# The beginning of a block kernel: tokens in two halves, and modulation in pieces between them

## The chip, the cores and the metric

The kernel runs on one core of a Trainium2 chip. The metric is the device time of one execution in microseconds (us); the number given for a kernel is the median of its runs. A core has five engines with a queue of instructions each, which are worked off in order: PE (TensorE, matrix products; its weight loads are shown apart as PEld), DVE (VectorE), ACT (ScalarE), POOL (GpSimd) and SP (SyncE, which here only issues DMAs). Engines wait for one another by semaphores.

## What is computed

One layer of a diffusion trunk, of 1024 latent tokens (a grid of 16 rows by 64 columns) and 256 context tokens, all of width 1024, in float32. Cut to what matters here:

```python
mod_x = silu(c) @ w_mod + b_mod           # six vectors of 1024: sh1, sc1, gt1, sh2, sc2, gt2
mod_c = silu(c_ctx) @ w_mod + b_mod
h_x = rmsnorm(x, g_pre_mix) * (1 + sc1) + sh1       # (1024, 1024)
h_c = rmsnorm(ctx, g_pre_mix) * (1 + csc1) + csh1   # (256, 1024)
u, q, k, v = split(h_x @ w_in)            # four times (1024, 512); k, v of h_c too
mix = concat(pool_mixer(u), neighbourhood_attention(q, k, v, k_c, v_c, rpb)) @ w_out
x = x + gt1 * rmsnorm(mix, g_post_mix)
y = square(relu((rmsnorm(x, g_pre_mlp) * (1 + sc2) + sh2) @ w_mlp_in)) @ w_mlp_out
out = x + gt2 * rmsnorm(y, g_post_mlp)
```

What is changed lies before the first products `h_x @ w_in`: the sums of squares and roots of `rmsnorm`, the turning of x so that its 1024 channels lie on the partitions, the product of `silu(c)` with the first two vectors' columns of `w_mod`, and the first of the sums for u.

## The kernel before

**Pieces.** A token tile `x0` to `x7` holds 128 tokens by 1024 channels. A channel chunk k (0 to 7) holds 128 channels on the partitions. `xT[k]` is chunk k of all 1024 tokens, in two halves b of 512 columns. The columns are ordered by grid tiles: (m, r, c), 8 tiles m of 16 rows by 8 columns; half b=0 holds grid tiles 0 to 3. In the memory the tokens are ordered by grid rows, so a token tile is two grid rows, and each half of `xT` needs all eight token tiles.

**Products** are made in three passes: weights and activations are split in a high part (type fp32r) and a low part (the rest), and high×high, low×high and high×low are summed (`some_sums`, L449). `hx[b][k]` holds both parts of the modulated half b of chunk k, 512 columns each. `pus[b][j]` is the bank in which the product for columns j (128 of u) and half b is summed over k.

**Steps in the beginning**, all in one order by hand: within `in_order` every engine keeps the order in which the program names the instructions.

- SP issues the loads: x0 to x7 (512 KB each, L293), then for each pair of chunks q (0 to 3) four pages `wm` of modulation weights (L300; 128 partitions with four runs of 1 KB) and a page of `w_in` (L178), then the context.
- `squares` (ACT, L131) sums the squares of a token tile; DVE adds epsilon (L136), POOL takes the root (L140), and DVE scales the tile in `normalised` (L334).
- PE turns 128 by 128 blocks (`turned`, L346) into banks `pxt`; ACT and DVE copy them into `xT` in the order of grid tiles (`by_bands`, L353). `spare` (L341) are transpositions of the unit matrix into a free place; nothing reads them.
- `mod_sums` (L401): the vector `sT` (32 columns, two of them used: c and c_ctx) times 256 columns of `w_mod` for shift and scale, the 1024 channels summed in four groups of 32 rows of the array, 32 instructions for a pair of chunks. `mod_kept` copies the row (ACT, L406), `shift_scale` picks it on PE with `pck` (L418) and makes the columns `a1` (scale) and `s1` (shift) on DVE (L422 to L427).
- `latent(b, k)` makes `hx` (`modulated`, L205 to L210): for b=0 ACT writes the high part, DVE the exact value and then the low part.
- The loop over q sums u for both chunks of a pair and both halves, and between them makes the next pair's modulation, weights and `hx`. For b=1 only columns j = 0, 1 are summed in it; j = 2, 3 come after the loop.

After the loop the context, k and v, pooling, attention, the output product and the MLP follow. They are long rows of matrix products; `stored_sum` (L519) adds quarters of the modulated `xT`, and the additions at L550 make it anew for k = 0 and 1 of half 0, since those two were modulated into another place.

**Banks.** PSUM has eight banks of 512 columns. `ps1` has six (tag `mm`), `ps_t` two (tag `T`, `lasting`). The function `bank` gives one of the two lasting ones to names that begin with `pm` and to a few others. A bank is given to a new name when every instruction that uses the old one is done.

Of the kernel before, what the change touches and what calls it, by code (L numbers as in the profile page):

```python
# [11 lines left out]
F32 = mybir.dt.float32  # L12
F32R = mybir.dt.float32r
# [5 lines left out]
P = 128  # L19
D = 1024  # L20
KT = D // P
# [48 lines left out]

def _pick_table():
# [9 lines left out]
def hybrid_block(ctx, tc, x, ctx_in, w_mod, b_mod, gp1, gp2, w_in, pool_w, rpb, w_out, w1, w2, vectors,  # L81
# [37 lines left out]
    tiles = lambda a: a.rearrange("(r m c) d -> m r c d", r=QR, m=NM)  # L119
# [151 lines left out]
    with tc.tile_pool(name="ps1", bufs=6, space=PSUM) as ps1, tc.tile_pool(name="tmp1", bufs=3) as tmp:  # L271

        def bank(name):
            if name[:2] == "pm" or name in ("pxt1_0", "pxt0_2", "pxt1_7", "pct2", "pct3"):
                return lasting(name)
            return ps1.tile([P, 512], F32, tag="mm", name=name)
# [20 lines left out]
        def mod_load(q, kh, w):  # L297
            src = w_mod[:, w * D + q * 256 : w * D + (q + 1) * 256].rearrange("(h k p) f -> h p k f", p=P, h=2)
            t = page(f"wm{q}_{kh}_{w}")
            nc.sync.dma_start(t.rearrange("p (k f) -> p k f", k=4), src[kh])  # L300
            return t

        xn = [token_tile(f"x{n}", x[n * P : (n + 1) * P, :]) for n in range(NT)]
        wm, raw_u = [], []
        for q in range(4):
            wm.append([[mod_load(q, kh, w) for w in range(2)] for kh in range(2)])
            raw_u.append(load(f"wu{q}", pair(w_in, q, 0, 512)))
# [17 lines left out]
        inverse = {}  # L325

        def squares(name, t):
            jk = page(f"jk{name}")
            ms = sm(f"ms_{name}", 1, 4)
            mean_square(jk, t, ms)  # L330
            inverse[name] = rsqrt_of(f"t_{name}", ms)

        def normalised(name, t):
            nc.vector.tensor_scalar_mul(t, t, inverse[name])  # L334

        xT = [None] * KT

# [5 lines left out]
        def turned(pts, ns, ks):  # L343
            for k in ks:
                for n in ns:
                    nc.tensor.transpose(pts[k][:, (n % 4) * P : (n % 4 + 1) * P], xn[n][:, k * P : (k + 1) * P], ident)  # L346

        def by_bands(copy, h, ks):
            for k in ks:
                if xT[k] is None:  # L350
                    xT[k] = page(f"xT{k}")
                to = xT[k].rearrange("p (m r c) -> p m r c", m=NM, r=QR)[:, :, 8 * h : 8 * h + 8]
                copy(to, pts[h][k].rearrange("p (r m c) -> p m r c", m=NM, c=QC))  # L353


        on_act, on_dve = nc.scalar.copy, nc.vector.tensor_copy
        pts = [{}, {0: bank("pxt1_0")}]
        free = pts[1][0][:, 3 * P :]

        def turned_in(h, ns, ks):  # L360
            for k in ks:
                if k not in pts[h]:
                    pts[h][k] = bank(f"pxt{h}_{k}")
            turned(pts[h], ns, ks)

        spare(free, 30)
        squares("x0", xn[0])
        for n in range(NT):
            if n + 1 < NT:
                squares(f"x{n + 1}", xn[n + 1])  # L370
            if n == 5:
                by_bands(on_dve, 0, (0,))
            if n == 7:
                by_bands(on_dve, 0, (1,))
            normalised(f"x{n}", xn[n])
            if n < 4:
                turned_in(0, (n,), range(KT - 1))
        spare(free, 3)
        turned_in(1, (4,), (0,))
        spare(free, 10)  # L380
        turned_in(0, (0, 1, 2, 3), (7,))
        turned_in(1, (5,), (0,))
        spare(free, 3)
        by_bands(on_dve, 0, (2,))
        by_bands(on_act, 0, (3, 4, 5, 6, 7))
        turned_in(1, (4, 5), (4, 5))
        turned_in(1, (6,), (0, 4, 5))
        turned_in(1, (4, 5, 6), (1,))
        turned_in(1, (7,), (0, 1, 4, 5))
        turned_in(1, (4, 5, 6, 7), (6,))  # L390
# [5 lines left out]
        def mod_sums(q, pm, kh):  # L396
            for k in range(4 * kh, 4 * kh + 4):
                for w in range(2):
                    c = 2 * (k % 2) + w
                    o = (k % 4) * 256  # L400
                    nc.tensor.matmul(pm[32 * c : 32 * c + 32, :256], sT[:, k, :], wm[q][kh][w][:, o : o + 256],  # L401
                                     start=(k < 2), stop=(k >= KT - 2))

        def mod_kept(q, pm):
            mr = tmp.tile([P, 256], F32, tag="mrow", name=f"mrow{q}", bufs=2)
            nc.scalar.copy(mr, pm[:, :256])  # L406
            return mr
# [6 lines left out]

        def shift_scale(q, mr):
            pt = bank(f"pmt{q}")
            for j in range(2):
                nc.tensor.matmul(pt[:, 4 * j : 4 * j + 4], mr[:, j * P : (j + 1) * P], pck, start=True, stop=True)  # L418
            pv = pt[:, :8].rearrange("p (j w v) -> p w v j", w=2, v=2)
            hs = slice(2 * q, 2 * q + 2)  # L420
            for v in range(2):
                nc.vector.tensor_tensor(a1[v][:, hs], pv[:, 1, v], b_sc[:, hs], add)  # L422
                nc.vector.tensor_tensor(a1[v][:, hs], a1[v][:, hs], g1c[:, hs], mul)
                if q < 2:
                    nc.vector.tensor_tensor(s1[v][:, hs], pv[:, 0, v], b_sh[:, hs], add)
                else:
                    nc.vector.scalar_tensor_tensor(s1[v][:, hs], pv[:, 0, v], -1.0, b_sh[:, hs], mul, sub)  # L427
# [3 lines left out]
        def latent(b, k):  # L431
            src = xT[k][:, b * 512 : (b + 1) * 512]
            h = page(f"hx{b}_{k}", F32R)
            modulated(tmp, f"hx{b}_{k}", src, a1[0][:, k : k + 1], s1[0][:, k : k + 1], h[:, :512], h[:, 512:], 512,
                      on_act=(b == 1), kept=src if b == 1 or k > 1 else None)
            hx[b][k] = h

# [4 lines left out]
        pus = [[bank(f"pu{j}_{b}") for j in range(4 if b == 0 else 2)] for b in range(2)]  # L442

        def some_sums(b, js, k):
            h = hx[b][k]
            hi, lo = h[:, :512], h[:, 512:]
            for n, (low, r) in enumerate(((0, hi), (1, hi), (0, lo))):
                for j in js:
                    nc.tensor.matmul(pus[b][j], wk(wgt, k, low, j * P, P), r,  # L449
                                     start=(k == 0 and n == 0), stop=(k == KT - 1 and n == 2))  # L450
# [12 lines left out]
        wu0h, wu0l = (whl.tile([P, 1024], F32R, tag="hl", name=f"wu0{n}") for n in "hl")  # L463
        by_bands(on_dve, 1, (0,))
        by_bands(on_act, 1, (1, 4, 5))
        by_bands(on_dve, 1, (6,))
        pm = bank("pm0")
        for kh in range(2):
            mod_sums(0, pm, kh)
        mr = mod_kept(0, pm)  # L470
        nc.scalar.copy(wu0h, raw_u[0])
        wgt.append((wu0h, wu0l))
        turned_in(1, (4, 5, 6, 7), (3,))
        shift_scale(0, mr)
        turned_in(1, (4, 5, 6, 7), (2, 7))
        nc.vector.tensor_tensor(wu0l, raw_u[0], wu0h.bitcast(F32), sub)
        latent(0, 0)
        latent(0, 1)
        by_bands(on_act, 1, (3, 2))
        by_bands(on_dve, 1, (7,))  # L480
        latent(1, 0)
        latent(1, 1)
        for q in range(4):
            some_sums(0, range(4), 2 * q)
            if q == 0:
                some_sums(0, (0, 1), 1)
            if q < 3:
                mr = mod_rows(q + 1)
                wgt.append(high_low(f"wu{q + 1}", raw_u[q + 1], 1.0 if q == 0 else -1.0))
            some_sums(0, range(2 if q == 0 else 0, 4), 2 * q + 1)  # L490
            if q < 3:
                shift_scale(q + 1, mr)
            for k in (2 * q, 2 * q + 1):
                some_sums(1, range(2), k)
            if q < 3:
                latents(q + 1)
            if q == 2:
                for i, t in enumerate(cp):
                    squares(f"c{i}", t)
                for i, t in enumerate(cp):  # L500
                    normalised(f"c{i}", t)
# [823 lines left out]
    with tc.tile_pool(name="ps2", bufs=6, space=PSUM) as ps2:  # L1325
# [6 lines left out]
      with ExitStack() as tmp2:  # L1332
# [565 lines left out]
        with tc.issue_after(first[ET.PE]), in_order(ET.PE, ET.Activation, ET.DVE, ET.SP):  # L1898
# [153 lines left out]
```

## Time and profile before

| | us |
|---|---|
| time, median of 3 runs (1027.45 to 1027.82) | 1027.65 |
| time of the profiled execution | 1028.11 |
| its span, first to last instruction | 1026.3 |
| PE busy in it | 1012.1 |
| first product `pu` starts | 23.18 |
| products of the loop over q done | 63.92 |
| last product starts | 1018.85 |

All times in the rows below are counted from the first instruction of the profiled execution. A row of a timeline reads: start, duration, engine, line, operation, tile written <- tiles read, shapes, how many instructions are merged in it, and in brackets how long the engine had been idle and for what it waited. Instructions of one engine overlap: the duration reaches to the end of the last one's result, and the next may start before. A row of waits reads: who waited for whom, us in total, times, longest. A row of windows reads: the window, its length, the busy time of PE, PEld, DVE, ACT and POOL with their numbers of instructions, the granted clock of PE, the share of the DMA engines and GB/s.

### The profile page before, as it was taken

The numbers are of one execution on the slowest core, as the hardware profiler recorded it, in microseconds if no ns is written. First come the engines' busy times: TensorE is split into PE (matmuls) and PEld (weight loads), VectorE is DVE, ScalarE is ACT, GpSimd is POOL, SyncE is SP. The second block draws the span as 40 slices with busy tenths as digits, with TensorE's granted clock in tenths as the row PEclk, the third lists the DMA queues.
The fourth block names the chain that finished last, engine by engine and source line by source line (L and its number), as shares of the span: only waits on it lengthen the run. The fifth ranks groups of instructions, "written<-read, shape, count | busy, mean of one in ns | idle before, by whom it ended". The sixth has DMA issues, their size and how long they took to land.

```text
span 1026.3 us, 16024 instructions
## 1 busy us (share of the span) xinstructions
PE 1012.1 (99%) x5910; PEld 839.0 (82%) x5910; DVE 746.8 (73%) x1156; ACT 546.0 (53%) x944; POOL 148.9 (15%) x230
## 2 busy tenths in 40 slices
PE   8999999999999999999999999999999999999997
PEld 6788888878898888888888888888888888888885
DVE  5588757977886688879998888755757666556576
ACT  7573254348896657776555554555543344334431
POOL 3011110156773321310000000000000000000001
PEclk9999999999999999999999999999999999999999
DMA  9999799623347966886776657537966766556556
GB/s 343 336 253 342 233 266 310 205 58 88 84 96 204 229 171 200 274 206 204 260 253 205 224 196 227 182 133 238 347 231 248 248 231 214 196 184 193 175 178 213
DMA packets 123134, 222.70 MB, mean 217 GB/s; under 512 B 9456, under 2 KB 55152, under 8 KB 123056
## 3 DMA queue, kind: packets, MB, share of 16 engines
q1 hardware_dynamic: 96560, 171.14, 50.7%
q0 software_dynamic: 9360, 19.58, 9.4%
q10 hardware_dynamic: 17136, 30.97, 8.1%
q8 instruction: 46, 0.75, 0.3%
q14 instruction: 32, 0.26, 0.1%
HBM read 168.16 MB, written 52.45 MB: 215 GB/s over the span
## 4 chain that ended last, share of the span: by engine, by line
PE 94%; DMA 2%; POOL 1%; ACT 1%; issue 1%; DVE 1%; SPq 0%; POOLq 0%; DVEq 0%; ACTq 0%
PE pu L449 4%; PE pa L1096 4%; PE phz L198 3%; PE phv L198 3%; PE pyx L198 3%; PE phx L198 3%; PE phx L200 3%; PE pyv L200 3%; PE pyx L200 3%; PE pyz L200 3%; PE pyv L199 3%; PE phz L199 3%; PE pyz L199 3%; PE phv L199 3%; PE phx L199 3%; PE phz L200 3%
## 5 line engine op out<-in xcount | busy, mean ns | idle before, releaser
L1042 ACT ACTIVATE sp<-sp,nm 128x640 f32<-128x640 f32 (+1 forms) x64 | 51.5, 805 | 9.6 <-DVE ri L1046 4.8
L1031 DVE CUSTOM_DVE_ANT_0 sp<-S,tab 128x640 f32<-128x640 f32 (+1 forms) x56 | 44.5, 794 | 14.1 <-PE pz L1062 10.3
L1638 ACT ACTIVATE c<-c 128x512 f32<-128x512 f32 x48 | 30.3, 631 | 45.9 <-DVE c L1758 25.7
L146 ACT CAST wpS<-S 128x512 fp32r<-128x512 f32 x64 | 38.8, 616 | 26.5 <-PE phv L200 9.9
L198 PE MATMUL phx<-thB,wpA 128*128 128x512 f32 x128 | 50.2, 392 | 0.0
L200 PE MATMUL phx<-thB,wpA 128*128 128x512 f32 x128 | 49.8, 389 | 0.0
L199 PE MATMUL phx<-tlB,wpA 128*128 128x512 f32 x128 | 49.8, 389 | 0.0
L152 DVE TENSOR_TENSOR wpS<-S,wpS 128x512 fp32r<-128x512 f32 x64 | 43.4, 685 | 7.6 <-ACT wpS L146 7.6
L140 POOL TENSOR_TENSOR ry<-vy,nhalf 128x1 f32<-128x1 f32 x8 | 5.9, 740 | 281.3 <-DVE vy L138 281.3
L1639 ACT ACTIVATE c<-c 128x512 f32<-128x512 f32 x48 | 30.3, 630 | 15.2 <-DVE sa L1721 12.1
L198 PEld LDWEIGHTS phx<-thB,wpA 128*128 128x128 f32 x128 | 24.0, 188 | 5.4 <-ACT s L1689 0.5
L200 PEld LDWEIGHTS phx<-thB,wpA 128*128 128x128 f32 x128 | 24.0, 188 | 5.0
L199 PEld LDWEIGHTS phx<-tlB,wpA 128*128 128x128 f32 x128 | 24.1, 188 | 4.8
L1081 DVE COPY pt<-T 128x512 f32<-128x512 f32 x32 | 21.9, 686 | 5.8 <-PE T L1062 5.8
L1096 PE MATMUL pa<-pt,v 128*64 128x128 f32 x352 | 25.9, 280 | 0.2
L198 PE MATMUL phz<-thB,wpS 128*128 128x512 f32 x64 | 25.0, 391 | 0.0
L198 PE MATMUL phv<-thT,wpA 128*128 128x512 f32 x64 | 25.0, 391 | 0.0
L199 PE MATMUL phz<-tlB,wpS 128*128 128x512 f32 x64 | 24.9, 390 | 0.0
L199 PE MATMUL phv<-tlT,wpA 128*128 128x512 f32 x64 | 24.9, 389 | 0.0
L200 PE MATMUL phz<-thT,wpS 128*128 128x512 f32 x64 | 24.9, 389 | 0.0
L200 PE MATMUL phz<-thB,wpS 128*128 128x512 f32 x64 | 24.9, 389 | 0.0
L200 PE MATMUL phv<-thT,wpA 128*128 128x512 f32 x64 | 24.9, 389 | 0.0
(1134 smaller groups left out, 3434.4 us busy)
## 6 DMA issues: line engine op xcount, KB each, us to landing
b<-in_w SPq DMA_DIRECT2D x64, 512.0 KB, 4.4
hrS<-hdS SPq DMA_DIRECT2D x32, 512.0 KB, 5.4
hrA<-hdA SPq DMA_DIRECT2D x24, 512.0 KB, 5.6
wm<-in_w_mod SPq DMA_DIRECT2D x16, 512.0 KB, 9.7
wa_0w<-in_w SPq DMA_DIRECT2D x16, 512.0 KB, 5.0
wa_1w<-in_w SPq DMA_DIRECT2D x16, 512.0 KB, 4.5
hdA<-c ACTq DMA_DIRECT2D x32, 256.0 KB, 2.9
hdS<-sa ACTq DMA_DIRECT2D x32, 256.0 KB, 3.2
```

The source lines that it names most:

```text
L146: nc.scalar.copy(hi, src)
L152: nc.vector.tensor_tensor(lo, src, hi.bitcast(F32), sub)
L198: nc.tensor.matmul(ps, ahi, bhi, start=first, stop=False, skip_group_check=more)
L199: nc.tensor.matmul(ps, ahi, blo, start=False, stop=False, skip_group_check=more)
L200: nc.tensor.matmul(ps, alo, bhi, start=False, stop=last, skip_group_check=more)
L449: nc.tensor.matmul(pus[b][j], wk(wgt, k, low, j * P, P), r, start=(k == 0 and n == 0), stop=(k == KT - 1 and n == 2))
L1031: nc.vector.tensor_tensor_reduce(out=to, in0=s, in1=bt, scale=1.0, scalar=BIG, op0=add, op1=ALU.min, accum_out=nm)
L1042: nc.scalar.activation(sp, sp, AF.Exp, bias=least[i, e], scale=-1.0, accum_out=sums[i][:, e : e + 1])
L1081: copy(turns[i].rearrange("p e i t -> p (e i) t")[:, :, h * HD : (h + 1) * HD], turned[i][h].rearrange("p (a t) -> p a t", a=8))
L1096: nc.tensor.matmul(pa[e * HD : (e + 1) * HD, cols], v[:, f : f + HD], turns[i][:, e, c] if c < 4 else fifths[i][:, :, (e + 1) * HD : (e + ...
L1638: nc.scalar.activation(r, src, AF.Relu)
L1639: nc.scalar.activation(r, r, AF.Square)
```

## The change

Tokens come in the order of grid tiles, both in the input and in the output; the host reorders them. So the first four token tiles are half b=0 and the last four half b=1, and copies into `xT` are plain (`put`). The host also packs the modulation weights into pages of 128 rows of 1024 numbers, `mod_pages`. For the first two pairs a page holds one chunk's shift and scale for half of the 1024 summed channels, so the row of a chunk can be made alone, in two halves of 16 instructions by 128 columns (`chunk_sums`), with its own pick (`picked`) and columns (`chunk_scale`, two instructions for each of c and c_ctx). The last two pairs keep the old form (`mod_rows`, `shift_scale`).

The loads are ordered x0 to x3, pair 0, x4 to x7, pair 1, pairs 2 and 3. PE sums chunk 0 of half 0 as soon as the four tiles are turned, with the modulation pieces of chunk 1 between its passes, then chunk 1; then come the squares, roots and transpositions of the second four tiles, through three banks `pxb` that take two chunks of two tiles each. Chunks 6 and 7 of the second half are turned later (`last_chunk`). The first high part of a weight is made on POOL. Chunks 0 and 1 of half 0 are modulated in place, and L550 is gone. `nc.sync.dma_start` for the output writes 128 consecutive rows.

```diff
-            if name[:2] == "pm" or name in ("pxt1_0", "pxt0_2", "pxt1_7", "pct2", "pct3"):
+            if name[:2] == "pm" or name in ("pxt5", "pxb2", "pxb3", "pxb4", "pct2", "pct3"):
                 return lasting(name)
...
+        def first_loads(q):
+            raw_u[q] = wraw.tile([P, 1024], F32, tag="raw", name=f"wu{q}w")
+            for i in range(2):
+                for kh in range(2):
+                    wm[q][i][kh] = mod_load(q, i, kh)
+                nc.sync.dma_start(raw_u[q][:, i * 512 : (i + 1) * 512], w_in[(2 * q + i) * P : (2 * q + i + 1) * P, :512])
+
+        xn = token_tiles(0)
+        first_loads(0)
+        xn += token_tiles(1)
+        first_loads(1)
...
+        def chunk_scale(k, pt, v):
+            ks = slice(k, k + 1)
+            nc.vector.scalar_tensor_tensor(a1[v][:, ks], pt[:, 2 + v : 3 + v], b_sc[:, ks], g1c[:, ks], add, mul)
+            nc.vector.tensor_tensor(s1[v][:, ks], pt[:, v : v + 1], b_sh[:, ks], add)
...
+        def latent_low(b, k):
+            h, src = hx[b][k], xT[k][:, b * 512 : (b + 1) * 512]
+            nc.vector.tensor_scalar(src, src, a1[0][:, k : k + 1], s1[0][:, k : k + 1], mul, add)
+            nc.vector.tensor_tensor(h[:, 512:], src, h[:, :512].bitcast(F32), sub)
...
+        pxt = [bank(f"pxt{k}") for k in range(5)] + [bank("pxt5"), bank("pxt6"), None]
...
+        def chunk_sums(k, kh):
+            if kh == 0:
+                whole[k] = bank(f"pm{k // 2}_{k % 2}")
+            mod_sums(k // 2, whole[k], kh, k % 2)
+
+        def chunk_row(k):
+            pt[k] = whole[k][:, 384:388]
+            return mod_kept(f"{k // 2}_{k % 2}", whole[k], P)
...
+        spare(free, 30)
+        squared(0)
+        rooted(0)
+        for n in range(4):
+            if n < 3:
+                squared(n + 1)
+                rooted(n + 1)
+            normalised(n)
+            if n == 2:
+                mod_sums(0, whole[0], 0, 0)
+            if n < 3:
+                first_turned(n, range(KT - 1))
+            if n < 2:
+                spare(free, 2)
+        mod_sums(0, whole[0], 1, 0)
+        mr = chunk_row(0)
+        first_turned(3, range(4))
+        picked(pt[0], mr, 0)
+        first_turned(3, range(4, KT - 1))
+        put(on_act, pxt[0], 0, 0)
+        half_weight(0, 0, lambda src, hi: nc.gpsimd.tensor_copy(hi, src))
+        chunk_scale(0, pt[0], 0)
+        put(on_dve, pxt[1], 1, 0)
+        latent_high(0, 0, on_act)
+        half_weight(0, 0, low_part)
+        latent_low(0, 0)
+        put(on_act, pxt[2], 2, 0)
+        put(on_act, pxt[3], 3, 0)
+        put(on_act, pxt[5], 5, 0)
+        put(on_dve, pxt[4], 4, 0)
+        put(on_dve, pxt[6], 6, 0)
+        chunk_scale(0, pt[0], 1)
+        chunk_sums(1, 0)
+        passes(0, range(4), 0, 0)
+        chunk_sums(1, 1)
+        mr = chunk_row(1)
+        half_weight(0, 1, high_part)
+        passes(0, range(4), 0, 1)
+        picked(pt[1], mr, 0)
+        chunk_scale(1, pt[1], 0)
+        latent_high(0, 1, on_dve)
+        half_weight(0, 1, low_part)
+        latent_low(0, 1)
+        passes(0, range(4), 0, 2)
+        pxt[7] = bank("pxt7")
+        for n in range(4):
+            first_turned(n, (7,))
+        squared(4)
+        put(on_act, pxt[7], 7, 0)
+        for n in range(5, NT):
+            squared(n)
+        some_sums(0, range(4), 1)
+
+        pxb = [bank(f"pxb{i}") for i in range(3)]
+        two = lambda k: pxb[k // 2][:, (k % 2) * 256 : (k % 2 + 1) * 256]
...
+        rooted(4)
+        chunk_scale(1, pt[1], 1)
+        rooted(5)
+        normalised(4)
+        rooted(6)
+        normalised(5)
+        rooted(7)
+        normalised(6)
+        for n in (4, 5):
+            second_turned(n, range(6))
+        chunk_sums(2, 0)
+        kept_two(on_act, (0, 2, 3, 4, 5), 4)
+        kept_two(on_dve, (1,), 4)
+        normalised(7)
+        second_turned(6, (0, 2, 3, 1, 4, 5))
+        second_turned(7, range(6))
+        chunk_sums(2, 1)
+        kept_two(on_act, (0,), 6)
+        latent_high(1, 0, on_act)
+        kept_two(on_dve, (1, 3), 6)
+        latent_low(1, 0)
+        kept_two(on_act, (2,), 6)
+        mr = chunk_row(2)
+        latent_high(1, 1, on_act)
+        half_weight(1, 0, high_part)
+        some_sums(1, range(2), 0)
+        picked(pt[2], mr, 0)
+        chunk_scale(2, pt[2], 0)
+        latent_low(1, 1)
+        latent_high(0, 2, on_act)
+        half_weight(1, 0, low_part)
+        latent_low(0, 2)
+        kept_two(on_act, (4,), 6)
+        kept_two(on_dve, (5,), 6)
+        chunk_scale(2, pt[2], 1)
         for kh in range(2):
...
+            chunk_sums(3, kh)
+        mr = chunk_row(3)
+        half_weight(1, 1, high_part)
+        some_sums(1, range(2), 1)
+        picked(pt[3], mr, 0)
+        chunk_scale(3, pt[3], 0)
+        half_weight(1, 1, low_part)
+        latent(1, 2)
+        chunk_scale(3, pt[3], 1)
+        some_sums(0, range(4), 2)
+        last_chunk(6)
+        latent(0, 3)
+        latent(1, 3)
+        some_sums(1, range(2), 2)
+        last_chunk(7)
+        mr = mod_rows(2)
+        wgt.append(high_low("wu2", raw_u[2], -1.0))
+        some_sums(0, range(4), 3)
+        shift_scale(2, mr)
+        some_sums(1, range(2), 3)
+        latents(2)
+        for q in (2, 3):
             some_sums(0, range(4), 2 * q)
...
-        for k in range(2):
-            hi, lo = hx[0][k][:, :512], hx[0][k][:, 512:]
-            nc.vector.tensor_tensor(xT[k][:, :512], hi.bitcast(F32), lo.bitcast(F32), add)
...
-                        nc.sync.dma_start(og[m][:, :, cs], xt[:, cs])
+                        nc.sync.dma_start(og[m][:, cs], xt[:, cs])
```

Names in it: `put` copies a bank's columns into `xT`; `second_turned(n, ks)` turns chunks ks of token tile n into `pxb`, and `kept_two(copy, ks, n)` copies there two tiles, n and n+1, of each chunk; `half_weight(q, i, part)` makes the high or low part of one chunk's weights; `passes(b, js, k, n)` is one of the three passes of `some_sums`.

More of the change, by code (lines that the diff above doesn't have):

```diff
@@ L116, in in_order @@
                 last[i.engine] = i
-    tiles = lambda a: a.rearrange("(r m c) d -> m r c d", r=QR, m=NM)
+    tiles = lambda a: a.rearrange("(m p) d -> m p d", p=P)
     xg, og = tiles(x), tiles(out)
@@ L294, in token_tile, with mod_load @@
             return t
[L297 to L300, printed above, removed]
-            return t
[L303 to L307, printed above, removed]
+        def mod_load(q, i, kh):
+            t = page(f"wm{q}_{i}_{kh}")
+            nc.sync.dma_start(t, mod_pages[4 * q + 2 * i + kh])
+            return t
+        token_tiles = lambda b: [token_tile(f"x{n}", x[n * P : (n + 1) * P, :]) for n in range(4 * b, 4 * b + 4)]
+        wm, raw_u = [[[None] * 2 for _ in range(2)] for _ in range(4)], [None] * 4
+        def first_loads(q):
+            raw_u[q] = wraw.tile([P, 1024], F32, tag="raw", name=f"wu{q}w")
+            for i in range(2):
+                for kh in range(2):
+                    wm[q][i][kh] = mod_load(q, i, kh)
[5 more added lines that the diff above has]
+        for q in (2, 3):
+            for kh in range(2):
+                for i in range(2):
+                    wm[q][i][kh] = mod_load(q, i, kh)
+            raw_u[q] = load(f"wu{q}", pair(w_in, q, 0, 512))
         cp = [token_tile(f"c{i}", ctx_in[i * P : (i + 1) * P, :]) for i in range(2)]
@@ L341, in spare @@
                 nc.tensor.transpose(ps, ident, ident)
[L343 to L353, printed above, removed]
@@ L356, in hybrid_block @@
-        on_act, on_dve = nc.scalar.copy, nc.vector.tensor_copy
[L357 to L390, printed above, removed]
+        def turned(to, n, k):
+            nc.tensor.transpose(to, xn[n][:, k * P : (k + 1) * P], ident)
@@ new lines, in put, with squared, rooted, normalised @@
+        def put(copy, src, k, n):
+            if xT[k] is None:
+                xT[k] = page(f"xT{k}")
+            copy(xT[k][:, n * P : n * P + src.shape[-1]], src)
+        on_act, on_dve = nc.scalar.copy, nc.vector.tensor_copy
+        means = {}
+        def squared(n):
+            means[n] = sm(f"ms_x{n}", 1, 4)
+            mean_square(page(f"jkx{n}"), xn[n], means[n])
+        def rooted(n):
+            means[n] = rsqrt_of(f"t_x{n}", means[n])
+        def normalised(n):
+            nc.vector.tensor_scalar_mul(xn[n], xn[n], means[n])
@@ L399, in mod_sums, with mod_kept @@
                     c = 2 * (k % 2) + w
[L400 to L406, printed above, removed]
+                    if i is None:
+                        src = wm[q][w][kh][:, (k % 4) * 256 : (k % 4 + 1) * 256]
+                    else:
+                        o = (2 * (k % 4) + w) * P
+                        src = wm[q][i][kh][:, o : o + P]
+                    nc.tensor.matmul(pm[32 * c : 32 * c + 32, :n], sT[:, k, :], src, start=(k < 2), stop=(k >= KT - 2))
+        def mod_kept(name, pm, n=256):
+            mr = tmp.tile([P, 256], F32, tag="mrow", name=f"mrow{name}", bufs=2)
+            nc.scalar.copy(mr[:, :n], pm[:, :n])
             return mr
@@ L413, in mod_rows, with picked @@
             return mod_kept(q, pm)
+        def picked(pt, mr, j):
+            nc.tensor.matmul(pt[:, 4 * j : 4 * j + 4], mr[:, j * P : (j + 1) * P], pck, start=True, stop=True)
         def shift_scale(q, mr):
@@ L434, in latent, with latent_high, passes @@
             modulated(tmp, f"hx{b}_{k}", src, a1[0][:, k : k + 1], s1[0][:, k : k + 1], h[:, :512], h[:, 512:], 512,
-                      on_act=(b == 1), kept=src if b == 1 or k > 1 else None)
+                      on_act=(b == 1 and k > 1), kept=src)
             hx[b][k] = h
+        def latent_high(b, k, copy):
+            h = hx[b][k] = page(f"hx{b}_{k}", F32R)
+            src, scale, shift = xT[k][:, b * 512 : (b + 1) * 512], a1[0][:, k : k + 1], s1[0][:, k : k + 1]
+            if copy is on_act:
+                nc.scalar.activation(h[:, :512], src, AF.Identity, bias=shift, scale=scale)
+            else:
+                nc.vector.tensor_scalar(h[:, :512], src, scale, shift, mul, add)
+        def latent_low(b, k):
+            h, src = hx[b][k], xT[k][:, b * 512 : (b + 1) * 512]
+            nc.vector.tensor_scalar(src, src, a1[0][:, k : k + 1], s1[0][:, k : k + 1], mul, add)
+            nc.vector.tensor_tensor(h[:, 512:], src, h[:, :512].bitcast(F32), sub)
         wgt = []
         up = [None] * 4
-        pus = [[bank(f"pu{j}_{b}") for j in range(4 if b == 0 else 2)] for b in range(2)]
-        def some_sums(b, js, k):
[L445 to L450, printed above, removed]
+        pus = [[], []]
+        def passes(b, js, k, n):
+            if not pus[b]:
+                pus[b] += [bank(f"pu{j}_{b}") for j in js]
+            low, r = ((0, hx[b][k][:, :512]), (1, hx[b][k][:, :512]), (0, hx[b][k][:, 512:]))[n]
+            for j in js:
+                nc.tensor.matmul(pus[b][j], wk(wgt, k, low, j * P, P), r,
+                                 start=(k == 0 and n == 0), stop=(k == KT - 1 and n == 2))
+        def some_sums(b, js, k):
+            for n in range(3):
+                passes(b, js, k, n)
         def kept_sums(b, j):
@@ L461, in latents @@
                     latent(b, k)
[L463 to L467, printed above, removed]
-        for kh in range(2):
[L469 to L483, printed above, removed]
+        wgt += [[whl.tile([P, 1024], F32R, tag="hl", name=f"wu{q}{n}") for n in "hl"] for q in range(2)]
+        def half_weight(q, i, part):
+            cs = slice(i * 512, (i + 1) * 512)
+            hi, lo = (t[:, cs] for t in wgt[q])
+            part(raw_u[q][:, cs], hi, lo) if part is low_part else part(raw_u[q][:, cs], hi)
@@ new lines, in hybrid_block, with first_turned @@
+        pxt = [bank(f"pxt{k}") for k in range(5)] + [bank("pxt5"), bank("pxt6"), None]
+        whole, pt = {}, {}
+        def chunk_sums(k, kh):
[5 more added lines that the diff above has]
+            return mod_kept(f"{k // 2}_{k % 2}", whole[k], P)
+        def first_turned(n, ks):
+            for k in ks:
+                turned(pxt[k][:, n * P : (n + 1) * P], n, k)
@@ new lines, in hybrid_block @@
+        whole[0] = bank("pm0_0")
+        free = whole[0][:, 128:256]
+        spare(free, 30)
[13 more added lines that the diff above has]
+        mod_sums(0, whole[0], 1, 0)
@@ new lines, in hybrid_block, with second_turned, kept_two @@
+        for n in range(4):
[7 more added lines that the diff above has]
+        two = lambda k: pxb[k // 2][:, (k % 2) * 256 : (k % 2 + 1) * 256]
+        def second_turned(n, ks):
+            for k in ks:
+                turned(two(k)[:, (n % 2) * P : (n % 2 + 1) * P], n, k)
+        def kept_two(copy, ks, n):
+            for k in ks:
+                put(copy, two(k), k, n)
@@ new lines, in last_chunk @@
+        def last_chunk(k):
+            ps = bank(f"pxb{k - 3}")
+            for n in range(4, NT):
+                turned(ps[:, (n - 4) * P : (n - 3) * P], n, k)
+            put(on_act, ps, k, 4)
+        rooted(4)
[10 more added lines that the diff above has]
+        kept_two(on_act, (0, 2, 3, 4, 5), 4)
@@ L497, in hybrid_block @@
             if q == 2:
[L498 to L501, printed above, removed]
+                xn += cp
+                for n in (8, 9):
+                    squared(n)
+                for n in (8, 9):
+                    rooted(n)
+                    normalised(n)
         def in_weights(name, raw, kk):
```

44 lines of the change are left out of this document (23 added, 21 removed).

## Prediction

> **What bounds the kernel now.** I read the page first, then the waits of TensorE (PE), the chain of waits over the first 100 us, and the engines' timelines there.
>
> ```profile
> span 1026.3 us, 16024 instructions
> ...
> PE 1012.1 (99%) x5910; PEld 839.0 (82%) x5910; DVE 746.8 (73%) x1156; ACT 546.0 (53%) x944; POOL 148.9 (15%) x230
> ...
> PE 94%; DMA 2%; POOL 1%; ACT 1%; issue 1%; DVE 1%; SPq 0%; POOLq 0%; DVEq 0%; ACTq 0%
> ```
>
> PE makes 94% of the chain that ends last. After 100 us it waits for others like this:
>
> ```profile
> PE pa L1062 <- POOL rb L1048: 1.8, 3, 0.8
> PE S L1016 <- DVE nm L1031: 0.3, 1, 0.3
> PE poz L198 <- DVE ns L1454: 0.3, 1, 0.3
> ```
>
> That is 2.4 us in 926, so a delay or a gain at the beginning reaches the end almost whole; the question is when PE gets through the beginning. As marker I take the start of the sums L449 for the columns left for later (`pu` with wu0 for j 2, 3, half b=1), which both programs issue after the same sums.
>
> ```profile
> 1.57 5.72 PE L341 MATMUL pxt<-ident 128*128 128x128 f32 x30 [1.57 <-POOL ident masks.py:199]
> 8.07 0.98 PE L346 MATMUL pxt<-ident,x 128*128 128x128 f32 x7 [0.77 <-DVE x L334]
> 9.29 0.98 PE L346 MATMUL pxt<-ident,x 128*128 128x128 f32 x7 [0.24 <-DVE x L334]
> ...
> 16.39 2.18 PE L346 MATMUL pxt<-ident,x 128*128 128x128 f32 x18 [0.69 <-DVE xT L353]
> ...
> 21.21 0.61 PE L418 MATMUL pmt<-cols,mrow 128*128 128x4 f32 x4
> ...
> 23.18 1.21 PE L449 MATMUL pu<-hx,wu0h 128*128 128x512 f32 x4 [0.43 <-ACT hx L208]
> ...
> 36.08 1.07 PE L449 MATMUL pu<-hx,wu1h 128*128 128x512 f32 x4
> 37.08 1.94 PE L401 MATMUL pm<-wm,sT 128*32 128x256 f32 x32
> 38.94 1.20 PE L449 MATMUL pu<-hx,wu1h 128*128 128x512 f32 x4
> ...
> 63.92 0.62 PE L449 MATMUL pu<-hx,wu0h 128*128 128x512 f32 x2
> ```
>
> These rows of PE's timeline (start, duration, line, tiles, count) give the prices. A transposition costs 2.18/18 = 0.12. A sum costs 0.228: four of them take the slots from 36.08 to 36.99. A modulation row of 32 instructions then takes 36.99 to 38.94, 1.95. Four picks take 0.34 of PE's time.
>
> From 8.07 to 63.92, 55.85 us, PE does 64 transpositions (7.7), four modulation rows (7.8), four times four picks (1.4) and 144 sums (32.8): 49.7 us of work. The other 6.2 are waits, spare transpositions and seams.
>
> **The change part by part.** *Loads.* Four tiles of x come first, then the first pieces of modulation.
>
> ```profile
> 5.00:10.00 5.00, 3.99 (x30) 3.52 (x28) 3.06 (x15) 4.61 (x10) 2.67 (x4) 1.00 1.03 420
> 20.00:24.00 4.00, 3.57 (x34) 2.55 (x27) 2.08 (x8) 3.01 (x5) 0.00 (x0) 1.00 1.09 356
> ```
>
> The last column is GB/s: 420 while x (4 KB rows) is loaded, 356 while modulation comes in 1 KB rows. The squares of x, which wait for it, show the same pace:
>
> ```profile
> 7.21 1.06 ACT L131 ACTIVATE jkx<-x 128x1024 f32<-128x1024 f32 x1
> ...
> 8.49 1.06 ACT L131 ACTIVATE jkx<-x 128x1024 f32<-128x1024 f32 x1
> ```
>
> The new pages have 4 KB rows, so I take 420: 0.524 MB in 1.25 us (1.47 if they stay at 356). x3 is there just ahead of 8.49, the first two pieces at 9.7 and 10.9 (9.9 and 11.4), needed at 10.4 and 12.0; all later ones have more room. DMA is priced at nothing; what hides it is PE's work before each piece.
>
> *Start.* ACT, DVE and POOL treat x0 to x3 as before, so transpositions of x0 start at 8.07 again. In order: x0 to 8.91, x1 to 10.13, spare ones to 10.4.
>
> *Pieces.* A row of 32 instructions by 256 columns becomes, for the first four chunks, two halves of 16 instructions by 128 columns, six halves apart and one chunk whole. None is in the trace; its bounds come from the row above and from the weight loads in it:
>
> ```profile
> 27.56 1.58 PEld L401 LDWEIGHTS pm<-wm,sT 128*32 128x32 f32 x32 [0.37 <-issue]
> ```
>
> If all scales with columns and count, a half costs 1.95/4 = 0.49. If no instruction gets cheaper by its columns, it costs 16 × 0.049 = 0.79 and the 0.37 around a row: 1.16. I take halved streaming with the fixed part whole, 0.40 + 0.37 = 0.77. The chunk that is whole costs 0.79 + 0.37 = 1.16. Together 6 × 0.77 + 1.16 = 5.8 against 3.9 for two old rows: 1.9 more (between 0 and 5.0).
>
> *First half.* So: half a piece to 11.1, x2 to 12.0, second half to 12.75, x3 (four) to 13.23, pick, three more to 13.8. The next piece needs a bank. `lasting` has two, held by `pm0_0` (until the second `chunk_scale(0)`, later) and `pxt5`. Its copy stands on ACT behind the row's copy, `put` 0, `latent_high`, `put` 2 and 3.
>
> ```profile
> 14.77 2.51 ACT L353 COPY xT<-pxt 128x512 f32<-128x512 f32 x5
> ...
> 20.78 0.37 ACT L406 COPY mrow<-pm 128x256 f32<-128x256 f32 x1 [1.27 <-PE pm L401]
> ...
> 22.31 1.52 ACT L208 ACTIVATE hx<-xT,s,a 128x512 fp32r<-128x512 f32 x2 [0.21 <-DVE s L425]
> ```
>
> A copy follows the one before after 0.48 and lands after 0.59, a `hx` after 0.71. Picks start at 13.25; by 21.21 against DVE's 21.85 below, less two picks, DVE has them 0.47 later, a1 and s1 are made by 14.0. Then ACT: `latent_high` 14.0, copies at 14.7, 15.2, 15.7, the last landing at 16.3. PE waits from 13.8 to 16.3: **2.5 us**. POOL's new copy of half a weight is hidden here if it takes under 2.8 us (raw there at 11.6, DVE's low part not before 14.4); POOL has half of
>
> ```profile
> 88.87 0.96 POOL L215 MEMSET accsh<- 128x1024 f32 x1 [24.82 <-DMA tokS<-xT]
> ```
>
> as its nearest row, 0.48, and even at several times that nothing is late.
>
> From 16.3 PE runs: half a piece, 4 sums, half a piece, 4 sums, pick, 4 sums, 4 transpositions, 12 sums, to 24.0. The root of x4 stands on DVE behind `latent_low(0, 1)` and starts about 22.7. How long a root takes is seen at the context:
>
> ```profile
> 58.88 0.15 DVE L136 TENSOR_SCALAR vt_c<-ms_c 128x1 f32<-128x1 f32 x1 [0.36 <-ACT jkc L131]
> ...
> 60.00 0.76 DVE L334 TENSOR_SCALAR c<-c,rt_c 128x1024 f32<-128x1024 f32 x1
> ```
>
> 1.1 to the scaling and 0.76 for it: x4 is ready at 24.6. PE waits 0.7, and 0.2 for x5. Then transpositions and two halves to 29.1, 0.3 for the copies that free the banks of `pxb0` and `pxb1`, 6 sums (0.1 waiting), pick until 31.07.
>
> *Fourth piece.* `chunk_sums(3)` needs a bank of `lasting` again. They are held by `pxb2`, free after `kept_two(on_dve, (5,), 6)`, and by `pm1_0`, free after `chunk_scale(2, ..., 1)`. Both stand on DVE's queue behind work that starts only with the pick: `chunk_scale(2, ..., 0)`, `latent_low(1, 1)`, the low part of half a weight, `latent_low(0, 2)`.
>
> ```profile
> 21.85 0.16 DVE L422 TENSOR_TENSOR a<-pmt,cols 128x2 f32<-128x2 f32 x1 [2.55 <-PE pmt L418]
> ...
> 23.66 0.54 DVE L209 TENSOR_SCALAR hx_0t<-xT,a,s 128x512 f32<-128x512 f32 x1
> 24.30 0.69 DVE L210 TENSOR_TENSOR hx<-hx_0t,hx 128x512 fp32r<-128x512 f32 x1
> 24.91 0.54 DVE L209 TENSOR_SCALAR hx_1t<-xT,a,s 128x512 f32<-128x512 f32 x1
> ...
> 82.10 0.42 DVE L695 TENSOR_TENSOR kcT<-kcT,pkc 128x256 f32<-128x256 f32 x1 [2.09 <-ACT kcT L694]
> ```
>
> A `latent_low` is 23.66 to 24.91, 1.25 us (1.2 where the two overlap better); a low part of 512 columns as the second row's slot, 0.6; a copy of 256 columns from a bank 0.42; the two small operations 0.2. That is 0.2 + 1.2 + 0.6 + 1.2 + 0.4 = 3.6, and 0.47 from the pick's start at 30.9: the bank is free at 35.0. PE waits **3.9 us** (3.5 to 4.2 by the spread of these rows). Behind `chunk_sums(3)` on PE stand all sums of chunk 1, half 1, whose operands have long been there.
>
> *Rest.* From 35.0 the whole piece (1.16), 114 sums (26.0), picks (0.8), 8 transpositions (1.0), two old rows (3.9) and 0.4 for the first `hx` of chunk 4: 68.3, 4.4 after the old marker. The same from the other side: 1.9 more for the pieces, and 8.1 of waits with 0.5 of spare transpositions where there were 6.2, 2.4 more.
>
> *Removed.* Two additions on DVE (L550) lie under sums: PE is busy 10.00 of 10 there, and DVE follows PE. Nothing. If PE were earlier instead, DVE could become the bound:
>
> ```profile
> 60.00:70.00 10.00, 10.00 (x55) 8.49 (x54) 9.56 (x17) 6.65 (x13) 3.83 (x3) 1.00 1.03 241
> 70.00:80.00 10.00, 10.00 (x50) 8.41 (x49) 10.00 (x17) 8.33 (x16) 0.00 (x0) 1.00 1.10 330
> ```
>
> (third busy column DVE). Output and the second reading of x move the same bytes in as many rows: nothing.
>
> The profiled execution took 1028.11 us (span 1026.3 and 1.8 around it), 0.46 above the runs' median of 1027.65. With 4.4 it comes to 1032.5, the median to **1032.0**.
>
> **The rivals.**
> (1) *The fourth piece finds its bank free.* Speaks for it: only the order of DVE decides, and the bank would be free once `pxb2` is copied before `latent_low(1, 1)`. Against: the order is written out and held. Then 4.4 − 3.9 = 0.5: 1028.2, no change.
> (2) *Faster.* The pieces cost 0.49 and neither bank is waited for: what decides is that both banks are free when PE asks, at 13.8 and 31.1. Then PE works from 8.07 on with 49.7 us and 0.5 of spare ones, and the marker comes at 58.3 plus 1.7 for the smaller waits, 60.0: 3.9 earlier, 1023.7. Against it: the two queues above. With the long wait alone gone and pieces at 0.49, the gain is 1.4.
> (3) *Pieces are no cheaper by the column.* Six halves at 1.16 and the whole one at 1.95 make 8.9 where I took 5.8: 3.1 more, 1035.1. For it: 49 ns from one instruction to the next may be the price of issuing two instructions. Against: four column groups stream beside each other at 256 columns.
> (4) *PE's clock falls in the 3.9 us.* The granted clock is 1.00 in all windows above, but PE's longest wait after 8 us is 0.8. From rest, at 1.57, 30 transpositions took 5.72, 2.1 more than at 0.12 each; the same loss once more gives 1034.1. The Trainium skill ("TensorE: Matmul & The Clock Gate", Part 1) says that an idle window of about 3.4 us, which runs freely, halves the clock until PE has been busy for as long; by it a wait of 3.9 us would sometimes hold a whole window. No run here shows it.
>
> **How the numbers follow.** Forecast 0.62, rival (1) 0.13, (2) 0.10, (3) 0.10, (4) 0.05. A measurement of this kernel tells about 0.2%, 2 us, from no change. Slower: forecast, (3) and (4), 0.77; same: (1), 0.13; faster: (2), 0.10. The forecast's own range is 1030.1 (pieces at 0.49: 1.9 less) to 1033.5 (bank waits and pieces half way to their upper ends). For 8 in 10 it goes from 1028.0, which takes in (1), to 1035.2, which takes in (3).
>
> **What would show it.** Right: first `pu` sums near 17 us instead of 23.18; then PE idle about 2.5 us ahead of the modulation instructions of the second chunk, released by an ACT copy, and about 3.9 us ahead of those of the fourth, released by DVE; the marker near 68. Sixteen modulation instructions from first to next work in 0.8 us. Wrong: no idle time ahead of the fourth piece, or a marker before 63.9.

## The result, and the profile after

| | before | changed |
|---|---|---|
| median, us | 1027.72 (6 runs, 1027.45 to 1028.10) | 1034.38 (6 runs, 1033.65 to 1036.07) |
| ratio | 1 | 1.0068, 95% interval 1.0055 to 1.0081 |
| profiled execution, us | 1028.11 | 1033.65 |
| its span | 1026.3 | 1031.9 |
| first product `pu` starts | 23.18 | 17.05 |
| marker (start of the sums left for later) | 63.92 | 71.01 |

The changed kernel is 6.7 us slower by the medians, inside the predicted range and 2.4 above the predicted time. PE's waits in the profile of the changed kernel (us in total, times, longest):

```profile
PE pm L402 <- issue: 3.7, 1, 3.7
PE pm L402 <- ACT xT L373: 2.4, 1, 2.4
PE pa L1213 <- POOL rb L1199: 1.8, 3, 0.8
```

Two new waits stand at the top, both ahead of modulation pieces (L402); the third was there before. PE's timeline shows where they lie:

```profile
10.40 0.65 PE L402 MATMUL pm<-wm,sT 128*32 128x128 f32 x16
10.98 0.99 PE L368 MATMUL pxt<-ident,x 128*128 128x128 f32 x7
...
13.17 0.52 PE L368 MATMUL pxt<-ident,x 128*128 128x128 f32 x3
16.05 1.08 PE L402 MATMUL pm<-wm,sT 128*32 128x128 f32 x16 [2.35 <-ACT xT L373]
17.05 2.08 PE L467 MATMUL pu<-hx,wu0h 128*128 128x512 f32 x4
19.06 0.65 PE L402 MATMUL pm<-wm,sT 128*32 128x128 f32 x16
...
31.92 0.28 PE L416 MATMUL pm<-cols,mrow 128*128 128x4 f32 x2
35.93 1.76 PE L402 MATMUL pm<-wm,sT 128*32 128x128 f32 x32 [3.72 <-issue]
37.62 1.22 PE L467 MATMUL pu<-hx,wu0h 128*128 128x512 f32 x2
38.64 1.05 PE L467 MATMUL pu<-hx,wu0l 128*128 128x512 f32 x2
...
71.01 0.62 PE L467 MATMUL pu<-hx,wu0h 128*128 128x512 f32 x2
```

For the longer wait the profile names no releaser ("issue"); DVE's timeline of the same execution does, by its times:

```profile
32.24 0.22 DVE L431 SCALAR_TENSOR_TENSOR a<-pm,cols 128x1 f32<-128x1 f32 x1 [0.94 <-PE pm L416]
32.38 0.15 DVE L432 TENSOR_TENSOR s<-pm,cols 128x1 f32<-128x1 f32 x1
32.44 0.54 DVE L453 TENSOR_SCALAR xT<-xT,a,s 128x512 f32<-128x512 f32 x1
33.01 0.69 DVE L454 TENSOR_TENSOR hx<-xT,hx 128x512 fp32r<-128x512 f32 x1
33.62 0.69 DVE L175 TENSOR_TENSOR wu1l<-wu1w,wu1h 128x512 fp32r<-128x512 f32 x1
34.22 0.54 DVE L453 TENSOR_SCALAR xT<-xT,a,s 128x512 f32<-128x512 f32 x1
34.80 0.69 DVE L454 TENSOR_TENSOR hx<-xT,hx 128x512 fp32r<-128x512 f32 x1
35.41 0.42 DVE L373 COPY xT<-pxb 128x256 f32<-128x256 f32 x1
```

DVE is busy from the pick on, and the copy that frees `pxb2` ends at 35.83; PE goes on at 35.93. There is more in PE's rows than the waits. Four sums take 0.91 of PE's time elsewhere, and about 1.1 right behind a piece (the first experiment below); the four at 17.05 take 2.01, up to 19.06, and the two at 37.62 take 1.02. The windows tell why; the column behind POOL's is the granted clock:

```profile
12.00:16.00 4.00, 1.69 (x25) 1.22 (x25) 2.62 (x7) 3.07 (x6) 0.61 (x1) 0.96 1.03 415
16.00:20.00 4.00, 3.95 (x38) 2.46 (x39) 1.41 (x5) 0.23 (x2) 0.00 (x0) 0.61 1.03 413
...
32.00:36.00 4.00, 0.28 (x7) 0.22 (x9) 3.69 (x10) 1.07 (x2) 0.00 (x0) 1.00 1.04 407
36.00:40.00 4.00, 4.00 (x38) 3.14 (x39) 0.02 (x1) 2.12 (x4) 0.00 (x0) 0.57 1.05 404
```

A clock of 0.57 over 4 us is 3.4 us at one half (0.43 × 4 / 0.5); 0.96 and 0.61 together are 3.4 us too. So each wait brings one stretch of 3.4 us at half the clock. Narrow windows, of the same execution, show where the clock falls:

```profile
15.50:15.75 0.25, 0.00 (x0) 0.00 (x0) 0.25 (x1) 0.25 (x2) 0.00 (x0) 0.86 1.00 410
36.00:36.25 0.25, 0.25 (x12) 0.25 (x16) 0.02 (x1) 0.00 (x0) 0.00 (x0) 0.82 1.03 410
1029.25:1029.50 0.25, 0.00 (x0) 0.00 (x0) 0.00 (x0) 0.00 (x0) 0.00 (x0) 0.88 1.01 369
```

The half clock begins 0.07, 0.09 and 0.06 us before the ends of these windows, at 15.68, 36.16 and 1029.44: the first 0.4 us before PE goes on at 16.05, the second 0.2 us after it goes on at 35.93, the third after the last product. DMA releases neither wait, and it moves 404 to 415 GB/s in all the windows of 4 us.

### The profile page after: what moved, and what is told of

Read it like the earlier page. It is cut to its first block, busy times and chain, and to the rows that moved or that the text cites. A ratio compares the mean times of both kernels' runs of the same rounds, so it can differ in the third digit from the quotient of the medians.

```text
span 1031.9 us, 16144 instructions
## 1 busy us (share of the span) xinstructions
PE 1014.0 (98%) x5962; PEld 839.8 (81%) x5962; DVE 747.8 (72%) x1164; ACT 544.2 (53%) x949; POOL 149.3 (14%) x231
## 4 chain that ended last, share of the span: by engine, by line
PE 95%; POOL 1%; ACT 1%; issue 1%; DVE 1%; DMA 0%; POOLq 0%; DVEq 0%; ACTq 0%
PE pu L467 4%; PE pa L1247 3%; PE phz L221 3%; PE phv L221 3%; PE phx L221 3%; PE pyx L221 3%; PE phx L223 3%; PE phz L223 3%; PE phv L223 3%; PE pyx L222 3%; PE pyx L223 3%; PE pyv L222 3%; PE pyv L221 3%; PE pyz L222 3%; PE pyz L221 3%; PE phx L222 3%
## 5 line engine op out<-in xcount | busy, mean ns | idle before, releaser
L221 PE MATMUL phy<-thT,wpS 128*128 128x512 f32 x64 | 24.9, 389 | 0.0
L222 PE MATMUL phy<-tlT,wpS 128*128 128x512 f32 x64 | 24.9, 389 | 0.0
```

The source lines that it names most:

```text
L221: nc.tensor.matmul(ps, ahi, bhi, start=first, stop=False, skip_group_check=more)
L222: nc.tensor.matmul(ps, ahi, blo, start=False, stop=False, skip_group_check=more)
```

## Experiments

All ratios are to the kernel before, measured on the same chip beside each run. Differences to the changed kernel are between medians that were taken apart from each other; the median of the kernel before lay between 1027.7 and 1028.0 beside them.

### The fourth piece's bank earlier

The copies that free `pxb2` go ahead of DVE's and ACT's work on the next parts.

```diff
-        kept_two(on_dve, (1, 3), 6)
+        kept_two(on_dve, (1, 3, 5), 6)
         latent_low(1, 0)
-        kept_two(on_act, (2,), 6)
+        kept_two(on_act, (2, 4), 6)
...
-        kept_two(on_act, (4,), 6)
-        kept_two(on_dve, (5,), 6)
```

> Theory: the bank of the fourth piece is late because two copies stand behind 3.5 us of DVE work, and the 3.7 us of PE idle time also halve PE's clock for 3.4 us. With both copies put ahead of that work the wait ahead of the fourth piece falls under 0.4 us and the second stretch at half clock is gone: 3.7 + 1.7 = 5.4 us faster than the changed kernel, about 1029. Rival: DVE is simply behind, the wait only moves to the sums of chunk 1 or chunk 2, whose low parts are no earlier; then less than 1.5 us is gained, 1033 or more.

Measured: 1027.23 (10 runs), ratio 1.000 (0.9991 to 1.0010): 7.1 us faster than the changed kernel where 5.4 were expected. PE's timeline of this kernel:

```profile
16.02 0.65 PE L402 MATMUL pm<-wm,sT 128*32 128x128 f32 x16 [2.35 <-ACT xT L373]
16.60 1.20 PE L467 MATMUL pu<-hx,wu0h 128*128 128x512 f32 x4
17.73 0.65 PE L402 MATMUL pm<-wm,sT 128*32 128x128 f32 x16
...
30.73 0.28 PE L416 MATMUL pm<-cols,mrow 128*128 128x4 f32 x2
30.94 1.08 PE L402 MATMUL pm<-wm,sT 128*32 128x128 f32 x32
31.95 0.74 PE L467 MATMUL pu<-hx,wu0h 128*128 128x512 f32 x2
...
38.80 1.93 PE L402 MATMUL pm<-wm,sT 128*32 128x256 f32 x32
40.67 1.21 PE L467 MATMUL pu<-hx,wu1h 128*128 128x512 f32 x4
...
64.49 0.62 PE L467 MATMUL pu<-hx,wu0h 128*128 128x512 f32 x2
```

The wait ahead of the fourth piece is gone and nothing takes its place: from the piece to the marker it is 33.6 us, against 35.1 in the changed kernel. So the rival, that DVE is simply behind, falls. The times point to a cause of the 1.7 us beyond what was expected: they fall in two groups, six from 1027.14 to 1027.25 and four from 1028.59 to 1028.85, with a mean clock of 0.998 in the lower group and 0.996 or 0.997 in the upper one. The profiled execution is one of the lower group, and in it the sums after the first wait run at full speed (1.13 us up to 17.73) although that wait is still 2.35 us. So the median counts the first stretch at half clock as gone too.

### The second piece's bank earlier

Chunk 5 of x3 is turned first, and DVE copies it at once.

```diff
-        first_turned(3, range(4))
+        first_turned(3, (5, 0, 1, 2))
         picked(pt[0], mr, 0)
-        first_turned(3, range(4, KT - 1))
+        first_turned(3, (3, 4, 6))
+        put(on_dve, pxt[5], 5, 0)
...
-        put(on_act, pxt[5], 5, 0)
```

> Theory: the second chunk's piece waits for one copy that is last of four on ACT. Chunk 5 of x3 is turned first and DVE copies it at once: the piece starts near 13.6 instead of 16.05, PE then waits about 0.5 us for the first hx and some tenths for banks, the first stretch at half clock is gone, and 3 us are gained of the 7.1 by which the marker is late: about 1031.4. Rival: the start is set by ACT's queue in any case (hx and the copies of chunks 2 and 3), so the sums start no earlier than 17 and less than 1 us is gained.

Measured: 1031.14 (6 runs), ratio 1.0032 (1.0020 to 1.0044), 3.2 us faster than the changed kernel, as expected. The waits of PE up to 75 us in this kernel:

```profile
PE pm L402 <- issue: 3.7, 1, 3.7
...
PE pm L402 <- DMA wm<-in_mod_pages: 0.4, 1, 0.4
```

In place of the 2.35 there are 0.4 us, for the piece's own load and not for the first `hx`, as was expected; the wait ahead of the fourth piece is untouched, and up to the last product the clock falls only behind that one, at 34.27.

### Spare work in both waits

The waits stay; PE fills them with transpositions of the unit matrix, which nothing reads.

```diff
         chunk_scale(0, pt[0], 0)
+        spare(free, 18)
...
         chunk_scale(2, pt[2], 0)
+        spare(whole[2][:, P : 2 * P], 25)
```

> Both waits stay; PE fills them with 18 and 25 spare transpositions, which nothing reads. Theory: the two stretches at half clock come from the idle time in the waits, and go: the clock stays at 1.00 up to the end, the runs lie closer together, and 3.2 us (1.5 + 1.7) are gained: about 1031. Rival: the clock falls for another reason (the kind of work after the waits), or its loss is hidden behind other waits: less than 0.5 us gained.

Measured: 1031.42 (6 runs, 1030.81 to 1031.67), ratio 1.0033 (1.0021 to 1.0046): 3.0 us faster than the changed kernel, with the waits as long as before (PE's timeline of this kernel):

```profile
13.81 2.19 PE L365 MATMUL pm<-ident 128*128 128x128 f32 x18
16.17 0.65 PE L402 MATMUL pm<-wm,sT 128*32 128x128 f32 x16 [0.17 <-ACT xT L373]
16.74 1.20 PE L467 MATMUL pu<-hx,wu0h 128*128 128x512 f32 x4
...
31.39 2.95 PE L365 MATMUL pm<-ident 128*128 128x128 f32 x25 [0.38 <-DVE s L432]
34.74 1.08 PE L402 MATMUL pm<-wm,sT 128*32 128x128 f32 x32 [0.41 <-PE pm L365]
```

The four sums after the first wait take 1.1 us again instead of 2.0, the fourth piece 1.0 instead of 1.7. The fourth piece even starts 1.2 us sooner than in the changed kernel, because its pick does. The granted clock of the profiled execution is 1.00 from 7 us on until after the last product. So idle time of PE halved the clock, and that alone cost 3 of the 6.7 us by the medians (2.2 between the two profiled executions, 2.8 at the marker).

### Spare work in the wait that the first edit left

```diff
         chunk_scale(0, pt[0], 0)
+        spare(free, 18)
```

on top of the edit on the fourth piece's bank.

> The edit on the fourth piece's bank, and 18 spare transpositions in the wait of 2.35 us ahead of the second piece, which stays. The edit alone gave ten times in two groups, six from 1027.14 to 1027.25 and four from 1028.59 to 1028.85. Theory: the upper group are executions in which the wait of 2.35 us still halved the clock for one stretch of 3.4 us; with spare work in it the upper group is gone and all times lie within 0.5 us, near 1027.2. Rival: the groups have another cause (DMA, the end), and both stay, 1.5 us apart.

Measured: 1027.21 (11 runs, 1027.16 to 1027.28), ratio 0.9994 (0.9985 to 1.0003). The upper group is gone. So the two groups were executions in which a wait of 2.35 us did or did not halve the clock.

### The order of the output alone

The kernel before, with stores of 128 consecutive rows that the host reorders.

```diff
-    xg, og = tiles(x), tiles(out)
+    xg, og = tiles(x), out.rearrange("(m p) d -> m p d", p=P)
...
-                        nc.sync.dma_start(og[m][:, :, cs], xt[:, cs])
+                        nc.sync.dma_start(og[m][:, cs], xt[:, cs])
```

> The kernel before with the order of the output alone changed (128 consecutive rows for each store, the host reorders). Theory: the end after the last product is 0.9 us shorter, as in the changed kernel, because each store is issued in 0.33 instead of 0.54 us and lands sooner; nothing else moves: about 1026.8. Rival: the shorter end belongs to something else in the changed kernel (the clock, the order of loads): no difference beyond 0.2 us.

Measured: 1027.15 (10 runs, 1026.38 to 1027.52) beside 1027.76 (23 runs, 1027.23 to 1028.29); ratio 0.9994 (0.9984 to 1.0003), which by itself does not part it from no change. The profile shows the place, though. The stores of the kernel before, and of this one:

```profile
L1947 SPq DMA_DIRECT2D out<-xo x9: 537/538/622, 1002.0 to 1022.2; - x9
...
DMA to landing us min/median/max: 2.8/3.7/4.9
```

```profile
L1952 SPq DMA_DIRECT2D out<-xo x9: 332/332/338, 1001.9 to 1022.1; - x9
...
DMA to landing us min/median/max: 2.0/2.6/4.9
```

The three numbers in the first line are ns to issue one store (least, median, most), then the times of the first and last. A store is issued in 0.33 instead of 0.54 us and lands 1.1 sooner (median); the last is issued at nearly the same time and the span is 1025.4 instead of 1026.3. The changed kernel has the same 332 ns and 2.6 us. The medians of the times lie 0.6 apart, not 0.9, and spans of the kernel before alone differ by 1.0; so the 0.9 is the difference between two profiled executions.

### Both banks earlier

The two edits on banks together.

> Both edits together (the copy that the second piece waits for, and the two that the fourth waits for, put ahead). Theory: the gains add as far as the second half lets them; with the first alone the start of half 1 came only 1 us sooner, since the squares and roots of x4 to x7 are then late. The marker comes near 63.5 against 63.9 before, no stretch at half clock; with the shorter end of 0.6 to 0.9 us about 1026.2, 1.5 us faster than before. Rival: a third wait for a bank or for the second half's roots takes all of it, and the time stays at that of the first edit on the fourth piece alone, 1027.2.

Measured: 1025.51 (11 runs, 1025.33 to 1025.83), ratio 0.9977 (0.9968 to 0.9986): 2.3 us faster than the kernel before, 8.9 faster than the changed one. PE's timeline:

```profile
13.87 0.65 PE L402 MATMUL pm<-wm,sT 128*32 128x128 f32 x16 [0.19 <-DMA wm<-in_mod_pages]
14.71 1.41 PE L467 MATMUL pu<-hx,wu0h 128*128 128x512 f32 x4 [0.20 <-issue]
...
29.22 0.28 PE L416 MATMUL pm<-cols,mrow 128*128 128x4 f32 x2
29.43 1.08 PE L402 MATMUL pm<-wm,sT 128*32 128x128 f32 x32
...
62.98 0.61 PE L467 MATMUL pu<-hx,wu0h 128*128 128x512 f32 x2
```

The marker comes 0.9 us ahead of the kernel before; in the profiled executions the end gives another 0.9, and 0.6 come from the attention stage (below). The gain on the edit of the fourth piece alone is 1.5 at the marker, half a microsecond more than expected, so no third wait took it.

## Why the prediction came out as it did

**The two waits: right.** The wait ahead of the second chunk's piece was put at 2.5 us from 13.8 to 16.3, behind ACT's fourth copy; it is 2.35, to 16.05, released by that copy. The wait ahead of the fourth piece was put at 3.9 us to 35.0, behind DVE's queue; it is 3.72, to 35.93. Moving three copies, and turning one chunk first, removes both but for 0.2 us.

**Loads, start, first sums: right.** The first sums start at 17.05 where "near 17" was written, and PE waits for no load. With an earlier piece the load is the next limit, 0.2 to 0.4 us.

**The pieces: a term that was mis-sized.** A half was put at 0.77 (0.49 to 1.16). It takes 0.58, from 10.40 to 10.98, the whole one 1.01 (30.94 to 31.95 at full clock). Six halves and the whole are 4.5 us, 0.6 more than two old rows by the price used, not 1.9.

**The clock: the step that failed.** The sum from the second piece on was made at full clock, and the fall of the clock was set aside as rival (4), with a chance of 0.05 and one loss of 2.1 us. It happened, and twice: spare work in the waits gives 3.0 us back. From 35.93 to the marker it is 35.1 us where the working had 33.3 (from 35.0 to 68.3). The 2.1 for one wait was taken from the start of the kernel; measured, one stretch costs 1.3 to 1.6 us: from the piece behind the wait to the next pick it is 4.62 us against 3.31 in the edit on the fourth piece, at the other wait 4.08 against 2.53, and the two groups of times lie 1.6 apart. The other wait, of 2.35 us, was not thought long enough at all. So the marker stands at 71.0, not at 68.3: about 2.9 us more for the clock, about 1.3 less for the pieces, and 1.1 in small seams (four sums behind another kind of work take 1.02 to 1.13 us and not 0.91), which were not added up one by one. The Trainium skill ("TensorE: Matmul & The Clock Gate", Part 1) gives a freely running window of about 3.4 us; the stretches of 3.4 us at half clock agree with it. It speaks of an idle window; the wait of 2.35 us, shorter than the window, halved the clock in some executions and not in others, and here the measurement decides.

The traces show what it goes with. The three falls in the profile of the changed kernel lie on a grid of 3.413 us: 6 steps from 15.68 to 36.16, 291 from there to 1029.44. In the slot ahead of the first (one step of the grid, 3.41 us) PE was idle for 2.0 us; ahead of the second, for 3.2. In the profile of the edit on the fourth piece the clock falls only after the last product:

```profile
1021.50:1021.75 0.25, 0.00 (x0) 0.00 (x0) 0.25 (x1) 0.00 (x0) 0.00 (x0) 0.96 0.00 0
```

That is at 1021.73, and 295 steps back from it a border lies at 14.80, inside the wait: 1.1 us of idle time on one side, 1.2 on the other, and no fall. In the eight profiled executions the clock fell behind every slot with 2.0 us or more of idle PE, and behind none with 1.5 us or less; between the two there is no case. By this, what a wait of 2.35 us costs hangs on where it falls on a grid that lies differently in each execution. No run was made to steer this.

**The end: a term put at nothing.** Of the 7.1 us at the marker 5.6 are left in the span. The order of the output was priced at nothing because the bytes and the rows are the same. With it the end, from the start of the last product on, takes 6.6 us instead of 7.5, 0.9 less, in this profile and in that of the output order alone; the stores are issued faster and land sooner. By the medians of that experiment it is 0.6, with an interval that reaches no change. The other 0.6 goes in the attention stage; the kernel before has one wait of PE there that the changed one has not (0.3, `poz` for DVE), and the rest of it was not traced.

**The sum.** 4.4 was forecast, 6.7 came. In the profiled executions 5.6 came: pieces 1.3 too dear, the clock 2.9 and the seams 1.1 too cheap, the end and attention 1.5 not seen. The other executions of the changed kernel go up to 1036.07 at a lower mean clock (0.993 against 0.996), so that the median lies 0.7 above the profiled one; that of the kernel before lies 0.4 below its own. That the time came out within 2.4 us is in part luck, since errors of 4.0 and 2.8 us stood against each other; it lies above the forecast's own range (1030.1 to 1033.5), and rival (4), at 1034.1, is nearest to it, but with one stretch of 2.1 us where there were two of 1.3 to 1.6.

## What to carry to other kernels

A bank, like any buffer, is free when its last reader in its own queue is done, so before a copy is ordered "by need", look up who wants its buffer next: here a copy of under half a microsecond, behind 3.2 us of work on its engine, cost PE a wait of 3.7 us and about 1.6 more by the clock. A wait of PE costs more than its length where the clock falls after it; if it can't be removed, spare work in it is worth having, and times that fall in two groups are a hint to look at the clock. A DMA's order of rows can have a price of its own at the end of a kernel, where nothing hides it; here it was 0.6 to 0.9 us, and the times alone do not part it from none.

## What was not expected of the hardware

The clock halved after a wait of PE of only 2.35 us, by the times in four of ten executions of one kernel, 1.6 us each, and with spare transpositions in the wait in none of eleven. In the profiled executions it fell after slots of 3.41 us in which PE had been idle for 2.0 us or more, and only after those. A store of 512 KB to consecutive rows was issued in 0.33 us instead of 0.54 and landed 1.1 us sooner (median) than one to 16 runs of 8 rows.
